# FFN1's up sets: one 512-column matmul per high weight block, with the main and cross halves added on DVE

## The chip, the core and the metric

The kernel runs on one NeuronCore of one Trainium2 chip. The metric is the device time of one execution in microseconds (us), as the median of several runs. Engine names are those of the profile: PE multiplies matrices and PEld loads its weights, DVE and ACT are the two elementwise engines that can read PE's accumulators, POOL and SP issue most of the DMAs.

## The reference

One transformer-like block on 512 tokens of width 1024, batch 1, float32: a first feed-forward layer (FFN1) with half weight, a mixer of a short causal convolution and a gated linear attention with their output projections, a second feed-forward layer (FFN2) with half weight, and a last normalisation. The part that the change concerns:

```python
D_MODEL, SEQ, D_FF = 1024, 512, 2816

def swiglu(x, w_gu, w_down):
    g, u = jnp.split(x @ w_gu, 2, axis=-1)
    return (jax.nn.silu(g) * u) @ w_down

x = x + 0.5 * swiglu(rmsnorm(x, norm_ffn1_g), ffn1_w_gu, ffn1_w_down)
x = x + hybrid_mixer(rmsnorm(x, norm_mix_g), w_in, conv_w, ...)
x = x + 0.5 * swiglu(rmsnorm(x, norm_ffn2_g), ffn2_w_gu, ffn2_w_down)
return rmsnorm(x, final_norm_g)
```

## The kernel before

**Numbers in two parts.** Every float32 operand of a matmul is split into a rounded high part and the remainder, the low part: ACT casts the value to the high part, DVE subtracts it from the value to get the low part. A product of two such operands is three matmuls into one accumulator: high weight by high operand, high weight by low operand, low weight by high operand. For weights the class `Weights` does this: a 128x1024 piece comes in by DMA (`f`), L358 casts it to `wh` on ACT, and L359 makes `wl` on DVE. `wh` and `wl` have 3 buffers each, so the cast for a product waits until the product three earlier has read its weights. L343 makes sums of weight pieces on DVE. For operands `Operands.make` does it (L599 on ACT, L600 on DVE).

**Sets.** Most large products are done in a Strassen-like way, with 7 half-size products instead of 8. A `Set` runs the products m1, p2, q6, p5, q7, p4 and p3. One product is 4 blocks of the contraction by 2 blocks of the output by the 3 matmuls above, 24 matmuls of 256 columns (L551) into one bank of the accumulator memory (PSUM). Bank b takes m1, q6, q7 and p4 one upon the other, bank a takes p2, bank c takes p5 and p3. After m1, q6 and q7 ACT copies bank b out (L556) before the next product adds into it. FFN1 and FFN2 have 9 such sets each in their up stage, with 4 pairs of plain column blocks ahead of them; the up stage's `done` then combines banks and copies on DVE (L715 after p2, L720 after q7, L724 after p4, L729 after p3). The down stages, the mixer's input projection and others use sets too, or plain runs of banks.

**Accumulators.** Eight banks in two pools: `ps` with 6 single banks given out by `MM()` (names `mm`), and `pa` with 2 given out by `AUX()` (names `aux`).

**What sets the order.** The program is written stage by stage; a scheduler of the framework then sets the order on each engine by its own cost estimates and adds the waits, from the tiles that an instruction reads and writes. A tile is the unit: an instruction that writes any part of a tile waits for earlier readers of any part of it. Only the last part of `last_down` is in written order (`manual_schedule`): for each of four token blocks t it runs `part(t, 0)` and `part(t, 1)`, 12 matmuls of 512 columns each (L833 to L835) into `o[t][0]` and `o[t][1]`, followed on DVE by the addition to the residual (L903), on ACT by squares, on DVE by the product with the last gain, and the store.

Of the kernel before, what the change touches and what calls it, by code (L numbers as in the profile page):

```python
# [78 lines left out]
HW = 256  # L79
# [136 lines left out]
def block_kernel(ctx: ExitStack, tc: tile.TileContext, xT, vecs, gf, gup, wgl, wts, out):  # L216
    nc = tc.nc
# [2 lines left out]

    front = ctx.enter_context(tc.tile_pool(name="front", bufs=1))
    keep = ctx.enter_context(tc.tile_pool(name="keep", bufs=1))
    ps = ctx.enter_context(tc.tile_pool(name="ps", bufs=6, space=bass.MemoryType.PSUM))
    pa = ctx.enter_context(tc.tile_pool(name="pa", bufs=2, space=bass.MemoryType.PSUM))

    cnt = [0]
# [11 lines left out]
    def tile_of(pool, shape, dtype=F32):  # L238
        cnt[0] += 1
        return pools[pool].tile(shape, dtype, tag=pool, name=f"{pool}{cnt[0]}")  # L240

    def T(dtype=F32):
        return tile_of("tp", [P, S], dtype)

    def MM():
        cnt[0] += 1
        return ps.tile([P, S], F32, tag="mm", name=f"mm{cnt[0]}")

    def AUX():
        cnt[0] += 1  # L250
        return pa.tile([P, S], F32, tag="aux", name=f"aux{cnt[0]}")
# [23 lines left out]
    class Weights:  # L275
# [3 lines left out]
        def __init__(self, ahead):  # L279
            self.ahead = ahead  # L280
            self.issued = 0
            self.taken = 0
            self.end = 0
            self.ready = []
            self.raw = {}
            self.loads = {}
            self.sums = {}
            self.pre = {}
# [88 lines left out]
    W = Weights(2)  # L377
# [145 lines left out]
    def mul(out_, a, b, eng=None):  # L523
        (eng or nc.vector).tensor_tensor(out=out_, in0=a, in1=b, op=ALU.mult)


    class Set:
# [8 lines left out]

        def run(self, p):
            b = {"m1": "b", "p2": "a", "q6": "b", "p5": "c", "q7": "b", "p4": "b", "p3": "c"}[p]
            fresh = b not in self.bank
            if fresh:  # L540
                self.bank[b] = MM()
            o = self.bank[b]
            bh, bl = self.group.get(p)
            h, l = W.take()
            for k in range(4):
                for e in range(2):
                    s = slice(k * HW + e * P, k * HW + (e + 1) * P)
                    t = slice(k * HW, (k + 1) * HW)
                    to = o[:, e * HW : (e + 1) * HW]
                    for j, (ww, aa) in enumerate(((h, bh), (h, bl), (l, bh))):  # L550
                        nc.tensor.matmul(to, ww[:, s], aa[:, t],  # L551
                                         start=fresh and k == 0 and e == 0 and j == 0,
                                         stop=k == 3 and j == 2, skip_group_check=True)
            if p in self.keep:
                v = T()
                nc.scalar.copy(v, o)  # L556
                self.v[p] = v
            self.done(self, p)

    class Operands:  # L560

        ORDER = ("m1", "p2", "p5", "q6", "q7", "p3", "p4")

        def __init__(self, b):
            self.b = b
            self.parts = {}
            self.sums = set()

# [19 lines left out]
        def make(self, p):  # L590
            if p in self.parts:
                return
            i = self.ORDER.index(p)
            if i > 0:
                self.make(self.ORDER[i - 1])
            v = self.sum(p)
            h, l = (tile_of("op", [P, 1024], F32R) for _ in range(2))
            hv, lv = (t.rearrange("p (k t) -> p k t", t=HW) for t in (h, l))
            nc.scalar.copy(hv, v)  # L599
            nc.vector.tensor_tensor(out=lv, in0=v, in1=hv.bitcast(F32), op=ALU.subtract)  # L600
            self.parts[p] = (h, l)
# [4 lines left out]
    class Tall:  # L606
# [7 lines left out]
        def run(self, p, s):  # L614
            b = {"p2": "a", "p5": "c", "p3": "c"}.get(p, "b")
            fresh = b not in self.bank
            if fresh:
                self.bank[b] = [MM(), MM()]
            bh, bl = self.group.get(p)
            h, l = W.take()  # L620
            for i in range(2):
                k = 2 * s + i
                wh, wl = (a[:, 512 * i : 512 * (i + 1)] for a in (h, l))
                for e in range(2):
                    c = slice(k * HW + e * P, k * HW + (e + 1) * P)
# [31 lines left out]
    def ffn(up, down, norm, nxt, plain, at):  # L657
# [7 lines left out]
        o = mm_group(up, KD, (0, DFF, P, DFF + P), xh, xl, extra=finish, slow=nxt is not None)  # L665
# [17 lines left out]
                xn[j, l] = v  # L683
            return xn[j, l]

        xo = Operands(normed)

        def plain_pair(f, g, u):
            s, t = T(), T()
# [9 lines left out]
        for f in range(2, plain):  # L699
# [5 lines left out]
                xo.sum("q6")  # L705
            plain_pair(f, g, u)

        def up_set(i):
            h = hid[:, plain + 2 * i : plain + 2 * i + 2]

            def done(s, p):
                bank, v = s.bank, s.v
                if p == "p2":
                    g1 = T()
                    nc.vector.tensor_tensor(out=g1, in0=bank["a"], in1=v["m1"], op=ALU.add)  # L715
                    nc.scalar.activation(g1, g1, AF.Silu)
                    s.g1 = g1
                if p == "q7":
                    u2 = T()
                    nc.vector.scalar_tensor_tensor(out=u2, in0=bank["c"], scalar=-1.0, in1=v["q7"],  # L720
                                                   op0=ALU.mult, op1=ALU.subtract)
                    s.u2 = u2
                if p == "p4":
                    nc.vector.scalar_tensor_tensor(  # L724
                        out=h[:, :, :HW], in0=pair(bank["b"]), scalar=-1.0, in1=pair(s.g1),
                        op0=ALU.mult, op1=ALU.mult)
                if p == "p3":
                    g2 = T()
                    nc.vector.tensor_tensor(out=g2, in0=bank["c"], in1=v["q6"], op=ALU.add)  # L729
                    nc.scalar.activation(g2, g2, AF.Silu)  # L730
                    mul(h[:, :, HW:], pair(s.u2), pair(g2))
                    if nxt is None and i < KD:
                        natural(i)

            return Set(xo, done)

        def pair(t):
            return t.rearrange("p (e t) -> p e t", t=HW)
# [13 lines left out]
            return last_down(us, hid, split_hid)  # L752

        def banks():
            return [AUX(), AUX()] + [MM() for _ in range(KD - 2)]

        def mm(d, k, w, hl):
# [10 lines left out]
        o = banks()  # L768
# [33 lines left out]
        o = banks()  # L802
# [17 lines left out]
    def last_down(us, hid, split_hid):  # L820
        X = XS[-1]
        gr = []
        for e in range(2):
            g = acc_row.tile([P, S], F32, tag=("acc", "row")[e], name=f"gr{e}")
            nc.sync.dma_start(g, gf[:, 512 * e : 512 * (e + 1)].to_broadcast([P, 512]))
            gr.append(g)

        o = [[MM(), MM()] for t in range(NTB - 1)] + [[AUX(), AUX()]]

        def mm(t, e, k, w, hl):  # L830
# [9 lines left out]
        def add(t, e, bank, by):  # L840
            xt = X[:, 4 * e : 4 * e + 4, t * P : (t + 1) * P]
            nc.vector.scalar_tensor_tensor(out=xt, in0=blocks(bank), scalar=by, in1=xt,
                                           op0=ALU.mult, op1=ALU.add)
# [25 lines left out]
        for p in CHUNK_ORDER:  # L869
            b = {"p2": "a", "p5": "c", "p3": "c"}.get(p, "b")  # L870
            fresh = b not in banks
            if fresh:
                banks[b] = [MM(), MM()]
            bh, bl = ho.get(p)
            for s in range(2):
                h, l = W.take()
                for i in range(2):
                    k = 2 * s + i
                    wh, wl = (a[:, 512 * i : 512 * (i + 1)] for a in (h, l))
                    for e in range(2):  # L880
                        c = slice(k * HW + e * P, k * HW + (e + 1) * P)
                        to = banks[b][e]
                        for n, (aa, ww) in enumerate(((bh, wh), (bh, wl), (bl, wh))):
                            nc.tensor.matmul(to, aa[:, c], ww,  # L884
                                             start=fresh and k == 0 and n == 0,
                                             stop=k == 3 and n == 2, skip_group_check=True)
            for l, e, by in uses[p]:
                for t in range(2):
                    add(2 * l + t, e, banks[b][t], by)
        o[:] = [[MM(), MM()] for t in range(NTB - 1)] + [[AUX(), AUX()]]  # L890
        w = [W.take(u) for u in us[KF - TAIL :]]
        hl = [split_hid(k) for k in range(KF - TAIL, KF, 2)]
# [41 lines left out]
        with tc.manual_schedule(engines={ENG.PE, ENG.DVE, ENG.Activation}):  # L934
# [4 lines left out]
            for t in range(NTB):  # L939
                sm = front.tile([P, 8], F32, tag="fin", name=f"fin{t}", bufs=2)  # L940
                f = [sm[:, i : i + 1] for i in range(6)]
# [563 lines left out]
```

## Time and profile before

| what | us |
|---|---|
| median of 3 runs (lowest, highest) | 1195.39 (1194.18, 1195.40) |
| the profiled execution's own time | 1195.04 |
| its span, first to last instruction | 1193.3 |
| PE busy in the span | 1183.7 |
| DVE busy | 841.7 |
| ACT busy | 591.7 |
| FFN1's up sets, from 50.46 to 232.43 | 181.97 |

The profile describes one execution, whose time was 1.74 us more than the span of its instructions. "Busy" adds up the instructions of an engine. A row of the timeline gives the start, the length, the engine, the line, the operation, the tiles written and read, and in brackets how long the engine sat idle before and what released it. Matmuls overlap in such rows, so the distance between the starts of two of them, not their length, tells what one costs. Buffer numbers are left out in the profile: `mm` is any bank of the pool `ps`.

### The profile page before, as it was taken

The page shows a single profiled execution, that of the slowest core. Times are in us where ns is not written, and L with a number is a line of the kernel's source. Part 1 is how long each engine was busy: PE and PEld are TensorE (multiplying, and loading weights), DVE is VectorE, ACT ScalarE, POOL GpSimd, SP SyncE. Part 2 cuts the span into 40 slices and gives each one's busy share as a digit, 9 for nine tenths or more (in the row PEclk, how much of TensorE's full clock was granted, in tenths as well). Part 3 has the DMA queues.
Part 4 walks back from the last instruction along what each step waited for, and adds up shares of the span by engine and source line. Part 5 has one row for each costly group of instructions (what it writes and reads, how often), then busy time and mean ns, then how long its engine had stood idle before and what let it go on. Part 6 is the DMA issues. An engine that isn't in the chain of part 4 may idle for free.

```text
span 1193.3 us, 19134 instructions
## 1 busy us (share of the span) xinstructions
PE 1183.7 (99%) x7834; PEld 1091.4 (91%) x7834; DVE 841.7 (71%) x1010; ACT 591.7 (50%) x736; POOL 106.4 (9%) x143
## 2 busy tenths in 40 slices
PE   9999999999999999999999999999999999999997
PEld 8899999988988889999999998888889999998886
DVE  7976666854787976667787786555597656675675
ACT  6554454622452746464554574334355555562353
POOL 0011111000110110101111100100001111100100
PEclk9999999999999999999999999999999999999999
DMA  9477777633482767778666766602637777763431
GB/s 345 82 210 183 189 177 190 182 89 90 99 278 72 172 158 208 196 185 212 143 152 147 189 172 214 203 18 78 213 81 211 170 184 173 185 174 117 92 92 70
DMA packets 58471, 190.80 MB, mean 160 GB/s; under 512 B 6576, under 2 KB 10800, under 8 KB 58384
## 3 DMA queue, kind: packets, MB, share of 16 engines
q1 hardware_dynamic: 36912, 124.27, 30.5%
q0 software_dynamic: 16832, 60.83, 27.5%
q10 hardware_dynamic: 4640, 4.49, 1.2%
q8 instruction: 61, 1.00, 0.3%
q14 instruction: 26, 0.21, 0.1%
HBM read 124.55 MB, written 8.39 MB: 111 GB/s over the span
## 4 chain that ended last, share of the span: by engine, by line
PE 97%; DVE 2%; issue 1%; ACT 0%; POOL 0%; DVEq 0%; ACTq 0%; POOLq 0%
PE mm L551 52%; PE mm L410 7%; PE mm L388 6%; PE mm L386 6%; PE mm L387 6%; PE mm L627 3%; PE mm L884 3%; PE mm L834 2%; PE mm L835 2%; PE mm L833 2%; PE aux L1173 1%; DVE wl L359 1%; PE aux L386 1%; PE aux L835 1%; PE aux L388 1%; PE aux L834 1%
## 5 line engine op out<-in xcount | busy, mean ns | idle before, releaser
L551 PE MATMUL mm<-op,wh 128*128 128x256 f32 x3584 | 648.8, 284 | 0.0
L358 ACT CAST wh<-f 128x1024 fp32r<-128x1024 f32 (+1 forms) x325 | 339.4, 1046 | 459.0 <-PE mm L551 221.8
L551 PEld LDWEIGHTS mm<-op,wh 128*128 128x128 f32 x3584 | 559.0, 192 | 1.1
L359 DVE TENSOR_TENSOR wl<-f,wh 128x1024 fp32r<-128x1024 f32 (+1 forms) x325 | 394.8, 1219 | 210.9 <-ACT wh L358 205.9
L551 PE MATMUL mm<-op,wl 128*128 128x256 f32 x1792 | 507.5, 283 | 0.9 <-DVE wl L359 0.9
L551 PEld LDWEIGHTS mm<-op,wl 128*128 128x128 f32 x1792 | 343.3, 192 | 1.6 <-DVE wl L359 1.5
L333 POOL DMA_DIRECT2D f<-f x108 | 93.4, 867 | 932.1 <-DVE wl L359 483.1
L386 PE MATMUL mm<-op,wh 128*128 128x512 f32 x340 | 132.3, 389 | 0.0
L387 PE MATMUL mm<-op,wh 128*128 128x512 f32 x340 | 132.3, 389 | 0.0
L388 PE MATMUL mm<-op,wl 128*128 128x512 f32 x340 | 132.3, 389 | 0.0
L387 PEld LDWEIGHTS mm<-op,wh 128*128 128x128 f32 x340 | 63.8, 188 | 13.3
L388 PEld LDWEIGHTS mm<-op,wl 128*128 128x128 f32 x340 | 63.8, 188 | 13.2
L386 PEld LDWEIGHTS mm<-op,wh 128*128 128x128 f32 x340 | 63.8, 188 | 13.2
L410 PE MATMUL mm<-op,wh 128*128 128x512 f32 x256 | 64.5, 394 | 0.0
L410 PEld LDWEIGHTS mm<-op,wh 128*128 128x128 f32 x256 | 48.6, 190 | 10.4
L556 ACT COPY tp<-mm 128x512 f32<-128x512 f32 x90 | 52.2, 580 | 2.0 <-DVE tp L1323 2.0
L599 ACT CAST op<-hid 128x1024 fp32r<-128x1024 f32 x28 | 29.4, 1051 | 37.4 <-PE aux L834 20.7
L600 DVE TENSOR_TENSOR op<-hid,op 128x1024 fp32r<-128x1024 f32 x28 | 34.2, 1222 | 17.7 <-ACT op L599 17.6
L343 DVE TENSOR_TENSOR f<-f,f 128x1024 f32<-128x1024 f32 x36 | 44.0, 1223 | 0.8
L627 PE MATMUL mm<-wh,op 128*128 128x512 f32 x112 | 34.9, 389 | 0.0
L884 PE MATMUL mm<-wh,op 128*128 128x512 f32 x112 | 34.6, 389 | 0.0
L410 PE MATMUL mm<-op,wl 128*128 128x512 f32 x128 | 34.2, 389 | 0.0
(252 smaller groups left out, 1107.7 us busy)
## 6 DMA issues: line engine op xcount, KB each, us to landing
f<-wts SPq DMA_DIRECT2D x219, 512.0 KB, 4.4
f<-f POOLq DMA_DIRECT2D x108, 512.0 KB, 5.0
X<-xT SPq DMA_DIRECT2D x8, 256.0 KB, 5.3
xs<-X POOLq DMA_DIRECT2D x8, 256.0 KB, 5.5
ga<-tp ACTq DMA_DIRECT2D x8, 256.0 KB, 5.3
gb<-tp ACTq DMA_DIRECT2D x8, 256.0 KB, 5.3
tp<-ga SPq DMA_DIRECT2D x8, 256.0 KB, 5.9
tp<-gb SPq DMA_DIRECT2D x8, 256.0 KB, 3.0
```

The costliest lines, as they stand in the source:

```text
L333: nc.gpsimd.dma_start(out_, a, accum_op=ALU.add)
L343: nc.vector.tensor_tensor(out=s3, in0=a11, in1=a21, op=ALU.add)
L358: nc.scalar.copy(h[:, :w], raw[:, :w])
L359: nc.vector.tensor_tensor(out=l[:, :w], in0=raw[:, :w], in1=h[:, :w].bitcast(F32), op=ALU.subtract)
L386: nc.tensor.matmul(o, wh, ah, start=first, stop=False)
L387: nc.tensor.matmul(o, wh, al, start=False, stop=False)
L388: nc.tensor.matmul(o, wl, ah, start=False, stop=last)
L410: nc.tensor.matmul(o[c], w[:, s : s + P], a[k], start=k == 0 and j == 0, stop=k == kt - 1 and j == 2)
L551: nc.tensor.matmul(to, ww[:, s], aa[:, t], start=fresh and k == 0 and e == 0 and j == 0, stop=k == 3 and j == 2, skip_group_check=True)
L556: nc.scalar.copy(v, o)
L627: nc.tensor.matmul(self.bank[b][e], aa[:, c], ww, start=fresh and i == 0 and n == 0, stop=k == 3 and n == 2, skip_group_check=True)
L884: nc.tensor.matmul(to, aa[:, c], ww, start=fresh and k == 0 and n == 0, stop=k == 3 and n == 2, skip_group_check=True)
```

## The change

In FFN1's up sets alone, an operand's high and low halves now lie beside each other, so that one matmul of 512 columns takes a high weight block to both of them. Its result is a main half (high by high) and a cross half (high by low), and the third matmul (low by high) adds into the cross half. A product is then 8 matmuls of 512 columns and 8 of 256, for each but p2, which keeps 24 matmuls of 256 columns in one bank of the pool `pa`. The accumulator of the others takes two banks. Where the kernel took bank b out by one ACT copy, `whole` now copies the cross half on ACT and adds the main half on DVE, after m1, q6, q7, and new after p4; after q7 and p3, where DVE combined one bank with a copy, it takes a second instruction for the cross half. That is six more DVE instructions of 512 elements and one more ACT copy for each set. An operand's split is done in two halves of 512 elements each instead of one piece of 1024.

The pool `ps` now has 3 tiles of two banks each instead of 6 of one. `MM2()` gives out such a tile, and `MM()`, which all other stages still call, gives out one half of a tile, then the other. The halves of one such tile are one tile to the waits.

```diff
-    ps = ctx.enter_context(tc.tile_pool(name="ps", bufs=6, space=bass.MemoryType.PSUM))
+    ps = ctx.enter_context(tc.tile_pool(name="ps", bufs=3, space=bass.MemoryType.PSUM))
...
+    half_bank = []
+
+    def MM2():
+        cnt[0] += 1
+        half_bank.clear()
+        return ps.tile([P, 2, S], F32, tag="mm", name=f"mm{cnt[0]}")
+
     def MM():
-        cnt[0] += 1
-        return ps.tile([P, S], F32, tag="mm", name=f"mm{cnt[0]}")
+        if half_bank:
+            return half_bank.pop()
+        t = MM2()
+        half_bank.append(t[:, 1])
+        return t[:, 0]
...
+        def run_joint(self, p, b):
+            fresh = b not in self.bank
+            two_banks = b != "a"
+            if fresh:
+                self.bank[b] = MM2() if two_banks else AUX()
...
+                    if two_banks:
+                        nc.tensor.matmul(o[:, e], h[:, s], a, start=fresh and k == 0,
+                                         stop=False, skip_group_check=True)
+                        nc.tensor.matmul(o[:, e, HW:], l[:, s], a[:, :HW], start=False,
+                                         stop=k == 3, skip_group_check=True)
+                        continue
...
+        def whole(self, b, v):
+            o = self.bank[b]
+            v = v.rearrange("p (e t) -> p e t", t=HW)
+            nc.scalar.copy(v, o[:, :, HW:])
+            nc.vector.tensor_tensor(out=v, in0=o[:, :, :HW], in1=v, op=ALU.add)
...
+            if self.joint:
+                t = [tile_of("op", [P, 1024], F32R) for _ in range(2)]
+                for i in range(2):
+                    a = t[i].rearrange("p (k b t) -> p k b t", b=2, t=HW)
+                    vi = v[:, 2 * i : 2 * i + 2]
+                    nc.scalar.copy(a[:, :, 0], vi)
+                    nc.vector.tensor_tensor(out=a[:, :, 1], in0=vi,
+                                            in1=a[:, :, 0].bitcast(F32), op=ALU.subtract)
...
                 if p == "q7":
-                    nc.vector.scalar_tensor_tensor(out=u2, in0=bank["c"], scalar=-1.0, in1=v["q7"],
+                    nc.vector.scalar_tensor_tensor(out=pair(s.u2), in0=main(bank["c"]),
...
+                    if xo.joint:
+                        nc.vector.tensor_tensor(out=pair(s.u2), in0=pair(s.u2),
+                                                in1=cross(bank["c"]), op=ALU.subtract)
                 if p == "p4":
...
+                    if xo.joint:
+                        s.whole("b", v["q7"])
...
+        half_bank.clear()
         o[:] = [[MM(), MM()] for t in range(NTB - 1)] + [[AUX(), AUX()]]
```

Three places show how the order of instructions moves. In the rows `op` tiles are operands, `wh` and `wl` are weights, `mm` and `aux` are accumulators, `tp` are copies in SBUF; the number in a name tells one tile from another, and a bracket names the engine whose earlier work the row waits for.

**FFN1's up sets, DVE.** Before, from the end of one set into the next:

```order
L359 TENSOR_TENSOR wl_1176<-f_908,wh_1175 128x1024
L720 SCALAR_TENSOR_TENSOR tp_1172<-mm_1104,tp_1170 128x512
L359 TENSOR_TENSOR wl_1207<-f_680,wh_1206 128x1024
L343 TENSOR_TENSOR f_1236<-f_1134,f_1138 128x1024
L724 SCALAR_TENSOR_TENSOR hid_353<-mm_946,tp_1039 128x2x256
L359 TENSOR_TENSOR wl_1240<-f_906,wh_1239 128x1024
L715 TENSOR_TENSOR tp_1267<-mm_1235,tp_1204 128x512
```

Now:

```order
L369 TENSOR_TENSOR wl_913<-f_415,wh_912 128x1024
L785 SCALAR_TENSOR_TENSOR tp_884<-mm_831,tp_881 128x512
L605 TENSOR_TENSOR tp_909<-mm_887,tp_909 128x512
L789 TENSOR_TENSOR tp_884<-tp_884,mm_831 128x512
L353 TENSOR_TENSOR f_936<-f_853,f_857 128x1024
L369 TENSOR_TENSOR wl_940<-f_666,wh_939 128x1024
L605 TENSOR_TENSOR tp_881<-mm_700,tp_881 128x512
L780 TENSOR_TENSOR tp_967<-aux_935,tp_909 128x512
L795 SCALAR_TENSOR_TENSOR hid_351<-tp_881,tp_780 128x2x256
```

Between the subtraction after q7 (L720 before, L785 now) and the addition after p2 (L715, L780) stand three more instructions of 512 elements: two additions of main halves (L605) and the second part of the subtraction (L789).

**FFN1's up sets, PE.** Before, each product is a run of 24 rows. Now the scheduler interleaves them: q6 and p5 as runs of 16, 5 rows of the next set's m1, q7's 16, the other 11 of m1, 8 rows of the next p2, p4's 16, the other 16 of p2, and p3's 16. The place where p2 begins, now:

```order
L585 MATMUL mm_1074<-op_357,wh_1019 128x512
L587 MATMUL mm_1074<-op_357,wl_1020 128x256
L593 MATMUL aux_1122<-op_372,wh_1075 128x256 [waits Activation_49]
L593 MATMUL aux_1122<-op_372,wh_1075 128x256
L593 MATMUL aux_1122<-op_372,wl_1076 128x256 [waits DVE_49]
```

The first two rows are the last of m1; p2's third row needs `wl_1076`, whose cast needs the weight buffer that q7 held until 11 rows earlier. Before, the 24 rows of m1 and the 24 of p4 stood between those two.

**The mixer's input sets, PE.** Before, at the start of a product that adds into a bank which ACT has to copy out first:

```order
L551 MATMUL mm_6363<-op_3898,wh_6286 128x256
L551 MATMUL mm_6363<-op_3899,wh_6286 128x256
L551 MATMUL mm_6363<-op_3898,wl_6287 128x256
L551 MATMUL mm_6105<-op_4258,wh_6331 128x256 [waits Activation_49]
L551 MATMUL mm_6105<-op_4259,wh_6331 128x256
```

Now, at a product with that same operand:

```order
L563 MATMUL mm_5463<-op_3776,wh_5597 128x256
L563 MATMUL mm_5463<-op_3777,wh_5597 128x256
L563 MATMUL mm_5463<-op_3776,wl_5598 128x256
L563 MATMUL mm_5780<-op_3565,wh_5720 128x256 [waits Activation_49]
L563 MATMUL mm_5780<-op_3566,wh_5720 128x256
L563 MATMUL mm_5463<-op_3883,wh_5681 128x256 [waits Activation_49]
L563 MATMUL mm_5463<-op_3884,wh_5681 128x256
```

Before, a whole product of 24 rows into another bank stands between the last row into `mm_6105` and the row that waits for its copy; now 2 rows stand there.

**The tail, PE.** The step from `part(1, 0)` to `part(1, 1)`, before:

```order
L833 MATMUL mm_11433<-op_11443,op_11451 128x512
L834 MATMUL mm_11433<-op_11444,op_11451 128x512
L835 MATMUL mm_11433<-op_11443,op_11452 128x512
L833 MATMUL mm_11434<-op_11397,op_11447 128x512 [waits PE_49]
L834 MATMUL mm_11434<-op_11398,op_11447 128x512
```

Now:

```order
L909 MATMUL mm_11004<-op_11012,op_11020 128x512
L910 MATMUL mm_11004<-op_11013,op_11020 128x512
L911 MATMUL mm_11004<-op_11012,op_11021 128x512
L909 MATMUL mm_11004<-op_10969,op_11016 128x512 [waits DVE_49]
L910 MATMUL mm_11004<-op_10970,op_11016 128x512
```

The two parts now write halves of one tile, and the second part's first row waits for DVE, which there reads the first part's half (the line that was L903 before).

More of the change, by code (lines that the diff above doesn't have):

```diff
@@ L538, in run @@
             b = {"m1": "b", "p2": "a", "q6": "b", "p5": "c", "q7": "b", "p4": "b", "p3": "c"}[p]
+            if self.group.joint:
+                return self.run_joint(p, b)
             fresh = b not in self.bank
@@ L558, in run, with __init__ @@
             self.done(self, p)
+        def run_joint(self, p, b):
[4 more added lines that the diff above has]
+            o = self.bank[b]
+            parts = self.group.get(p)
+            h, l = W.take()
+            for k in range(4):
+                a = parts[k // 2][:, (k % 2) * S : (k % 2 + 1) * S]
+                for e in range(2):
+                    s = slice(k * HW + e * P, k * HW + (e + 1) * P)
+                    if two_banks:
[4 more added lines that the diff above has]
+                        continue
+                    to = o[:, e * HW : (e + 1) * HW]
+                    for j, (ww, aa) in enumerate(((h, a[:, :HW]), (h, a[:, HW:]),
+                                                  (l, a[:, :HW]))):
+                        nc.tensor.matmul(to, ww[:, s], aa, start=k == 0 and e == 0 and j == 0,
+                                         stop=k == 3 and j == 2, skip_group_check=True)
+            if p in self.keep:
+                v = T()
+                self.whole(b, v)
+                self.v[p] = v
+            self.done(self, p)
+        def whole(self, b, v):
+            o = self.bank[b]
+            v = v.rearrange("p (e t) -> p e t", t=HW)
+            nc.scalar.copy(v, o[:, :, HW:])
+            nc.vector.tensor_tensor(out=v, in0=o[:, :, :HW], in1=v, op=ALU.add)
     class Operands:
         ORDER = ("m1", "p2", "p5", "q6", "q7", "p3", "p4")
-        def __init__(self, b):
+        def __init__(self, b, joint=False):
             self.b = b
+            self.joint = joint
             self.parts = {}
@@ L596, in make @@
             v = self.sum(p)
+            if self.joint:
[6 more added lines that the diff above has]
+                                            in1=a[:, :, 0].bitcast(F32), op=ALU.subtract)
+                self.parts[p] = t
+                return
             h, l = (tile_of("op", [P, 1024], F32R) for _ in range(2))
@@ L684, in normed @@
             return xn[j, l]
-        xo = Operands(normed)
+        xo = Operands(normed, joint=nxt is not None)
         def plain_pair(f, g, u):
@@ L706, in ffn, with main, cross @@
             plain_pair(f, g, u)
+        def main(t):
+            return t[:, :, :HW] if xo.joint else pair(t)
+        def cross(t):
+            return t[:, :, HW:]
         def up_set(i):
@@ L718, in done @@
                 if p == "q7":
-                    u2 = T()
-                    nc.vector.scalar_tensor_tensor(out=u2, in0=bank["c"], scalar=-1.0, in1=v["q7"],
+                    s.u2 = T()
+                    nc.vector.scalar_tensor_tensor(out=pair(s.u2), in0=main(bank["c"]),
+                                                   scalar=-1.0, in1=pair(v["q7"]),
                                                    op0=ALU.mult, op1=ALU.subtract)
-                    s.u2 = u2
+                    if xo.joint:
+                        nc.vector.tensor_tensor(out=pair(s.u2), in0=pair(s.u2),
+                                                in1=cross(bank["c"]), op=ALU.subtract)
                 if p == "p4":
-                    nc.vector.scalar_tensor_tensor(
-                        out=h[:, :, :HW], in0=pair(bank["b"]), scalar=-1.0, in1=pair(s.g1),
-                        op0=ALU.mult, op1=ALU.mult)
+                    b = pair(bank["b"]) if not xo.joint else pair(v["q7"])
+                    if xo.joint:
+                        s.whole("b", v["q7"])
+                    nc.vector.scalar_tensor_tensor(out=h[:, :, :HW], in0=b, scalar=-1.0,
+                                                   in1=pair(s.g1), op0=ALU.mult, op1=ALU.mult)
                 if p == "p3":
                     g2 = T()
-                    nc.vector.tensor_tensor(out=g2, in0=bank["c"], in1=v["q6"], op=ALU.add)
+                    nc.vector.tensor_tensor(out=pair(g2), in0=main(bank["c"]), in1=pair(v["q6"]),
+                                            op=ALU.add)
+                    if xo.joint:
+                        nc.vector.tensor_tensor(out=pair(g2), in0=pair(g2), in1=cross(bank["c"]),
+                                                op=ALU.add)
                     nc.scalar.activation(g2, g2, AF.Silu)
@@ L754, in banks @@
         def banks():
+            half_bank.clear()
             return [AUX(), AUX()] + [MM() for _ in range(KD - 2)]
@@ L826, in last_down @@
             gr.append(g)
+        half_bank.clear()
         o = [[MM(), MM()] for t in range(NTB - 1)] + [[AUX(), AUX()]]
@@ L872, in last_down @@
             if fresh:
+                half_bank.clear()
                 banks[b] = [MM(), MM()]
@@ L889, in last_down @@
                     add(2 * l + t, e, banks[b][t], by)
+        half_bank.clear()
         o[:] = [[MM(), MM()] for t in range(NTB - 1)] + [[AUX(), AUX()]]
```

## The prediction

> **What bounds the kernel now.** I read the page's engine sums and its chain first, then the groups, then the stage in which the matmuls change.
>
> ```profile
> PE 1183.7 (99%) x7834; PEld 1091.4 (91%) x7834; DVE 841.7 (71%) x1010; ACT 591.7 (50%) x736; POOL 106.4 (9%) x143
> PE 97%; DVE 2%; issue 1%; ACT 0%; POOL 0%; DVEq 0%; ACTq 0%; POOLq 0%
> L551 PE MATMUL mm<-op,wl 128*128 128x256 f32 x1792 | 507.5, 283 | 0.9 <-DVE wl L359 0.9
> L358 ACT CAST wh<-f 128x1024 fp32r<-128x1024 f32 (+1 forms) x325 | 339.4, 1046 | 459.0 <-PE mm L551 221.8
> L359 DVE TENSOR_TENSOR wl<-f,wh 128x1024 fp32r<-128x1024 f32 (+1 forms) x325 | 394.8, 1219 | 210.9 <-ACT wh L358 205.9
> ```
>
> PE is the bound all along: its rows fill 99% of the span, 97% of the chain is PE, and the one wait on DVE in the third row cost 0.9 us in the whole run. So a matmul saved is time saved, and every new wait of PE is time lost at full price. The last two rows show who feeds it: a cast of 1.05 us and a subtraction of 1.22 us for each weight piece. The stage itself, and two slices of it:
>
> ```profile
> core 0: us, PE busy (x) PEld busy (x) DVE busy (x) ACT busy (x) POOL busy (x), PEclk, DMA share, GB/s
> 50.46:232.43 181.97, 181.79 (x1514) 181.52 (x1512) 128.13 (x129) 98.21 (x118) 21.55 (x25) 1.00 0.74 184
> 50.46:70.60 20.14, 19.96 (x165) 19.69 (x164) 19.75 (x20) 14.03 (x17) 3.10 (x4) 1.00 0.72 184
> 90.80:111.00 20.20, 20.20 (x171) 20.20 (x170) 12.91 (x14) 9.86 (x12) 2.59 (x3) 1.00 0.75 183
> ```
>
> A set takes 20.2 us; DVE is busy for 12.9 of that in a steady set, but for 19.75 of 20.14 in the first one. The granted clock is 1.00 throughout.
>
> **The saving.** The price of a matmul is the distance of starts:
>
> ```profile
> 50.46 0.40 PE L551 MATMUL mm<-op,wh 128*128 128x256 f32 x2
> 50.69 0.28 PE L551 MATMUL mm<-op,wl 128*128 128x256 f32 x1
> 50.81 0.40 PE L551 MATMUL mm<-op,wh 128*128 128x256 f32 x2
> ...
> 1166.97 0.39 PE L833 MATMUL mm<-op,op 128*128 128x512 f32 x1
> 1169.69 0.39 PE L833 MATMUL mm<-op,op 128*128 128x512 f32 x1
> ```
>
> Three matmuls of 256 columns take 50.81 - 50.46 = 0.35 to 0.36, 0.12 each; the last two rows are 12 matmuls of 512 columns apart, 2.72 / 12 = 0.2267 each. Merging two of 256 into one of 512 saves 0.24 - 0.2267 = 0.0133. There are 9 sets x 6 products x 8 = 432 merges: 5.76 us. The stage's matmuls fall from 63 x 2.88 = 181.44 to 54 x 2.773 + 9 x 2.88 = 175.68.
>
> The Trainium skill ("TensorE: Matmul & The Clock Gate", section "Back-to-back issue gap") gives N/2.4 + 2.5 ns for N columns at the warm clock: 109.2 ns for 256, 215.8 for 512. By it a merge saves only 2.5 ns, all of them 1.1 us, and the sum below would be 4.7 us higher. This case's rows read 120 and 226.7, so I keep the rows.
>
> **What the up sets lose.** Distances that I need:
>
> ```profile
> 76.91 0.40 PE L551 MATMUL mm<-op,wh 128*128 128x256 f32 x2
> 77.04 1.05 ACT L358 CAST wh<-f 128x1024 fp32r<-128x1024 f32 x1 [1.36 <-PE mm L551]
> 77.11 0.69 DVE L729 TENSOR_TENSOR tp<-mm,tp 128x512 f32<-128x512 f32 x1 [0.69 <-PE mm L551]
> 78.00 0.63 ACT L730 ACTIVATE tp<-tp 128x512 f32<-128x512 f32 x1
> 78.12 1.23 DVE L359 TENSOR_TENSOR wl<-f,wh 128x1024 fp32r<-128x1024 f32 x1 [0.32 <-ACT wh L358]
> ...
> 57.03 0.39 PE L551 MATMUL mm<-op,wl 128*128 128x256 f32 x1 [0.18 <-DVE wl L359]
> 57.25 0.40 PE L551 MATMUL mm<-op,wh 128*128 128x256 f32 x2
> ```
>
> A product ends at 76.91, where the next starts: the cast into its buffer begins 0.13 later, DVE's read of its bank 0.20 later; `wl` begins 0.03 after the cast's end (78.09 to 78.12). When PE waits for `wl`, its next matmul comes 0.22 after the late one instead of 0.12, so I count 0.14 from DVE's end to PE at speed.
>
> Steady sets: DVE gets six operations of 0.69 more, 12.9 + 4.1 = 17.0 of some 20 us, which fits on average, as does ACT's one copy more. But p2's third matmul now waits for a chain that starts at q7's end: 0.13 + 1.05 + 0.03 + 1.23 + 0.14 = 2.58, and PE has 11 rows of m1 (5 x 0.2267 + 6 x 0.12 = 1.85) and two of p2 (0.24) to cover it: 0.49 lost in each of six sets, with some 0.1 more for q7, whose bank must now pass a copy and an addition. That is 3.4. A late set adds about 1.3, where p4 stands directly behind 11 rows and needs copy and addition behind a weight subtraction. First set: DVE is full before the change (19.75 of 20.14) and gets 4 us of work more, so up to 4 are lost; I take 3.0, since the additions after p4 and p3 fall into the next slice, where DVE has 7 us free. Sum lost 7.7; the 0.5 that PE lost here before goes. Stage: 175.7 + 7.7 = 183.4 against 181.97, **+1.4** (bounds -2.5, if the first set recovers and the steady chain hides, and +4).
>
> **What the pairs of banks cost elsewhere.** FFN1's down sets: the second product into a bank now stands 2 rows behind the first, and waits until DVE's addition has read it.
>
> ```profile
> 300.24 1.22 DVE L359 TENSOR_TENSOR wl<-f,wh 128x1024 fp32r<-128x1024 f32 x1
> 301.37 0.69 DVE L796 SCALAR_TENSOR_TENSOR X<-mm,X 128x512 f32<-128x512 f32 x1
> 300.61 0.40 PE L551 MATMUL mm<-op,wh 128*128 128x256 f32 x2
> ```
>
> The first product ended at 300.61, where its successor starts, and the addition, behind a `wl`, at 302.06: 302.06 + 0.14 - 300.61 - 0.24 = 1.35. The sets after it have 8 rows of cover, 0.07 each. At FFN1's end, three pairs of plain banks finish one behind the other, and one of them waits for its twin's addition: 0.20 + 0.69 + 0.14 = 1.03, as in the tail below. With 0.2 for the small ones, **+2.6** (1.3 to 3.5).
>
> Mixer and FFN2: at four places in the mixer's sets, and two in FFN2's up sets, 0 or 2 rows stand where a whole product stood between the last matmul into a bank and the next one that adds into it. PE then waits for ACT's copy, which stands in ACT's order behind a cast that gets ready at the same moment:
>
> ```profile
> 620.87 1.05 ACT L358 CAST wh<-f 128x1024 fp32r<-128x1024 f32 x1 [1.78 <-PE mm L551]
> 621.83 0.58 ACT L556 COPY tp<-mm 128x512 f32<-128x512 f32 x1
> ```
>
> From the cast's start to the copy's end it is 622.41 - 620.87 = 1.54, with 0.13 ahead and 0.14 behind 1.81; less 2 rows, 1.57. If the cast were done, it is 0.20 + 0.58 + 0.14 = 0.92, less 0.24: 0.68. Mixer: 1.57 twice and 1.81 twice is 6.8, low 3.2; nearer the high end, because the quoted rows show that very pair back to back. I take 5.5 with some 0.5 of small ones in it. FFN2: 2 x 1.57, low 1.4; I take 2.6. The output projections and single banks, which now share a tile two by two, wait some 8 times for a read of the twin (1.03 as in the tail), of which rows into other banks cover all but about 0.1: 0.8. Together **+8.9** (5.2 to 11.4).
>
> The tail: `part(t, 1)` waits for DVE's reading of `part(t, 0)` for t = 0, 1, 2.
>
> ```profile
> 1167.17 0.69 DVE L903 SCALAR_TENSOR_TENSOR X<-mm,X 128x512 f32<-128x512 f32 x1 [2.03 <-PE mm L835]
> 1167.90 0.69 DVE L524 TENSOR_TENSOR tp<-X,gr 128x512 f32<-128x512 f32 x1
> ```
>
> `part(0, 0)` ended at 1166.97; 0.20 + 0.69 + 0.14 = 1.03 each, three times **+3.1**, with nothing to cover it: PE is in written order there and ends the program. t = 3 has its own tiles and keeps its pace. The order of SP and POOL is unchanged, so the transfers cost nothing new; casts that move with PE's products only move their issue along.
>
> **Sum.** 1195.0 (the profiled execution; the median is 0.35 higher) + 1.4 + 2.6 + 8.9 + 3.1 = 1211.0. The bounds add to -2.5 + 1.3 + 5.2 + 3.1 = +7.1 and 4 + 3.5 + 11.4 + 3.2 = +22.1.
>
> **Rivals.** (1) The pairs' waits hide, because DVE and ACT come to their reads earlier than I read from the trace of before, and the up sets keep the saving: only the tail's 3.1 stays, 1195.0 - 5.8 + 3.1 = 1192.3, or 1189.3 if even the tail's read came in time. For it: DVE is idle 29% of the span. Against: a read cannot start before the product's end plus 0.20, and the tail row was released by PE itself, so 0.92 to 1.03 stands wherever no row covers it. The point at which it decides: fewer than 5.8 us of waits in all. (2) The up sets give back just the saving and elsewhere all copies find their engine free: 1195 + 0 + 1.3 + 5.2 + 3.1 = 1204.6. (3) DVE becomes the bound of the up sets: if each set's DVE work (17.0) is in the order of the products' needs and not free to slide, each addition queues behind a `wl` of 1.22, twice a set, 9 x 2 x 1.22 = 22 minus what I have counted (7.7) = 14 more: 1225. Against it: 3 us a set are idle. (4) The merge saves only the 1.1 us of the page's rule: 1215.7. Against it: the rows' 0.0133.
>
> **Chances.** My sum, within its range of 1204 to 1217: 0.72. Rival 2 and what lies near it down to 1198: 0.08. Rival 4 and moderate queueing, 1217 to 1221: 0.08. Rival 3: 0.05. Rival 1: 0.05, and 0.02 for ends within 0.2% (2.4 us) of before, which is about what a measurement of this kernel can tell from no change. Slower 0.93, same 0.02, faster 0.05. The predicted time is 1210.5, half a microsecond under the sum, since a wait that lets DVE catch up spares the next. Range 1202 to 1219.
>
> **What the profile after would show.** Starts of 512- and 256-column rows alternating at 0.2267 and 0.12 in the up sets; a stage of 181 to 186 us, its first set the longest; PE idle of 15 to 25 us in the whole run, put down to DVE additions and ACT copies outside the up sets; in the tail three gaps of 1.0 us ahead of `part(t, 1)` and none for t = 3. I am wrong if PE idles for less than 8 us, or if the stage ends under 178 us.

## The result, and the profile after

The changed kernel takes 1224.16 us (median of 4 runs, 1223.46 to 1224.57) against 1194.95 for the kernel before beside it: a ratio of 1.0245, 95% interval 1.0227 to 1.0262. It is slower by 29.2 us. The forecast was slower, at 1210.5 in a range of 1202 to 1219: the direction was right, and the size was about half of what came.

The page of the profiled execution (1223.91 us, span 1222.2), its sums by engine and its chain:

```profile
PE 1191.9 (98%) x7402; PEld 1067.6 (87%) x7402; DVE 869.5 (71%) x1071; ACT 597.8 (49%) x752; POOL 106.2 (9%) x143
PE 89%; DVE 5%; ACT 3%; DMA 2%; issue 2%; SPq 0%; ACTq 0%; DVEq 0%
```

PE has 432 matmuls fewer and its busy time is 8 us longer, so busy time tells little here. The chain tells more: PE's share fell from 97% to 89%, and DVE and ACT stand in it with 8%. PE's waits, with what ended them (total us, times, longest):

```profile
PE mm L563 <- ACT wh L368: 6.1, 6, 1.6
PE mm L909 <- DVE X L981: 2.4, 3, 0.8
PE mm L585 <- DVE tp L605: 2.3, 2, 1.3
PE mm L563 <- ACT tp L568: 2.2, 2, 1.5
PE aux L593 <- DVE wl L369: 1.4, 6, 0.2
...
PE mm L396 <- DVE y L534: 1.1, 1, 1.1
PE mm L686 <- DVE wl L369: 1.1, 1, 1.1
PE aux L593 <- ACT wh L368: 1.0, 1, 1.0
PE mm L420 <- DVE X L838: 0.9, 1, 0.9
PE mm L398 <- DVE wl L369: 0.7, 1, 0.7
```

L585, L587 and L593 are the matmuls of FFN1's up sets, where the change was made. Most of the waits are at other lines: L563 is the set matmul of the mixer, of FFN1's down and FFN2's up stage, L909 the tail. In windows by stage, before:

```profile
core 0: us, PE busy (x) PEld busy (x) DVE busy (x) ACT busy (x) POOL busy (x), PEclk, DMA share, GB/s
232.43:297.74 65.31, 65.31 (x291) 54.06 (x290) 34.19 (x34) 18.92 (x20) 3.45 (x4) 1.00 0.37 101
297.74:338.05 40.31, 40.31 (x338) 40.31 (x337) 29.24 (x32) 16.54 (x16) 3.44 (x5) 1.00 0.48 124
432.76:712.25 279.49, 278.29 (x2247) 272.86 (x2246) 206.78 (x257) 158.36 (x206) 29.75 (x38) 1.00 0.69 176
886.85:1071.75 184.90, 184.90 (x1546) 184.89 (x1545) 126.95 (x128) 101.97 (x126) 21.52 (x25) 1.00 0.74 182
1164.25:1193.30 29.05, 21.92 (x97) 17.83 (x95) 17.41 (x46) 9.54 (x24) 0.00 (x0) 0.91 0.19 72
```

And after:

```profile
50.45:236.57 186.12, 181.05 (x1083) 158.60 (x1082) 156.34 (x185) 102.25 (x130) 21.51 (x25) 1.00 0.71 179
236.57:301.42 64.85, 64.85 (x288) 53.68 (x287) 36.31 (x36) 19.96 (x21) 3.44 (x4) 1.00 0.40 106
301.42:343.42 42.00, 40.98 (x337) 40.57 (x336) 28.82 (x32) 16.44 (x16) 3.44 (x5) 1.00 0.44 108
440.66:727.85 287.19, 280.72 (x2248) 273.60 (x2246) 207.78 (x260) 158.76 (x206) 29.66 (x38) 1.00 0.67 171
906.12:1099.29 193.17, 190.16 (x1554) 187.34 (x1553) 128.95 (x131) 102.26 (x126) 21.50 (x25) 1.00 0.71 178
1189.81:1222.20 32.39, 22.89 (x97) 17.60 (x95) 17.81 (x46) 9.54 (x24) 0.00 (x0) 0.96 0.17 66
```

The up sets and the banks behind them (which interlock by two rows after) take 250.97 instead of 247.28, **+3.7**. FFN1's down sets: **+1.7**. From their end to the mixer's sets 97.24 instead of 94.71, **+2.5**. The mixer's sets: **+7.7**. From their end to FFN2's sets 178.27 instead of 174.60, **+3.7**. FFN2's sets: 193.17 holds 9 rows of the next stage (9 x 0.227 = 2.0), so **+6.2**. The banks after them +0.1, and the tail **+3.3**. That is 28.9, the difference of the spans. Only 3.7 of it lie where the arithmetic was changed.

### The profile page after: what moved, and what is told of

It is laid out like the page before. It is cut to its first block, busy times and chain, and to the rows that moved or that the text cites. A ratio compares the mean times of both kernels' runs of the same rounds, so it can differ in the third digit from the quotient of the medians.

```text
span 1222.2 us, 18379 instructions
## 1 busy us (share of the span) xinstructions
PE 1191.9 (98%) x7402; PEld 1067.6 (87%) x7402; DVE 869.5 (71%) x1071; ACT 597.8 (49%) x752; POOL 106.2 (9%) x143
## 4 chain that ended last, share of the span: by engine, by line
PE 89%; DVE 5%; ACT 3%; DMA 2%; issue 2%; SPq 0%; ACTq 0%; DVEq 0%
PE mm L563 36%; PE mm L420 7%; PE mm L585 7%; PE mm L396 6%; PE mm L398 6%; PE mm L397 6%; PE mm L587 3%; PE mm L961 3%; PE mm L686 3%; DVE wl L369 2%; ACT wh L368 2%; PE aux L593 2%; PE mm L909 2%; PE mm L911 2%; PE mm L910 2%
## 5 line engine op out<-in xcount | busy, mean ns | idle before, releaser
L563 PE MATMUL mm<-op,wh 128*128 128x256 f32 x2576 | 471.2, 285 | 9.9 <-ACT wh L368 6.1
L563 PEld LDWEIGHTS mm<-op,wh 128*128 128x128 f32 x2576 | 401.8, 191 | 16.2 <-ACT wh L368 8.8
L563 PE MATMUL mm<-op,wl 128*128 128x256 f32 x1288 | 361.9, 283 | 0.6 <-DVE wl L369 0.6
L563 PEld LDWEIGHTS mm<-op,wl 128*128 128x128 f32 x1288 | 245.3, 191 | 1.0 <-DVE wl L369 0.8
L585 PE MATMUL mm<-op,wh 128*128 128x512 f32 x432 | 152.7, 398 | 2.7 <-DVE tp L605 2.3
L396 PE MATMUL mm<-op,wh 128*128 128x512 f32 x340 | 132.5, 392 | 1.1 <-DVE y L534 1.1
L398 PE MATMUL mm<-op,wl 128*128 128x512 f32 x340 | 132.2, 390 | 0.7 <-DVE wl L369 0.7
L397 PE MATMUL mm<-op,wh 128*128 128x512 f32 x340 | 132.4, 389 | 0.0
L587 PE MATMUL mm<-op,wl 128*128 128x256 f32 x432 | 119.4, 280 | 0.0
L585 PEld LDWEIGHTS mm<-op,wh 128*128 128x128 f32 x432 | 81.0, 188 | 22.4 <-DVE tp L605 3.0
L587 PEld LDWEIGHTS mm<-op,wl 128*128 128x128 f32 x432 | 81.5, 189 | 0.5
L396 PEld LDWEIGHTS mm<-op,wh 128*128 128x128 f32 x340 | 63.8, 188 | 17.0 <-DVE y L534 2.4
L398 PEld LDWEIGHTS mm<-op,wl 128*128 128x128 f32 x340 | 63.8, 188 | 14.6 <-DVE wl L369 1.1
L397 PEld LDWEIGHTS mm<-op,wh 128*128 128x128 f32 x340 | 63.8, 188 | 12.9
L420 PE MATMUL mm<-op,wh 128*128 128x512 f32 x256 | 64.4, 391 | 1.3 <-DVE X L838 0.9
L420 PEld LDWEIGHTS mm<-op,wh 128*128 128x128 f32 x256 | 47.7, 188 | 12.4 <-issue 1.3
L658 DVE TENSOR_TENSOR op<-hid,op 128x1024 fp32r<-128x1024 f32 x21 | 25.6, 1221 | 18.5 <-ACT op L657 18.5
L568 ACT COPY tp<-mm 128x512 f32<-128x512 f32 x63 | 36.5, 579 | 2.2 <-DVE tp L1401 1.7
```

The costliest lines, as they stand in the source:

```text
L396: nc.tensor.matmul(o, wh, ah, start=first, stop=False)
L397: nc.tensor.matmul(o, wh, al, start=False, stop=False)
L398: nc.tensor.matmul(o, wl, ah, start=False, stop=last)
L420: nc.tensor.matmul(o[c], w[:, s : s + P], a[k], start=k == 0 and j == 0, stop=k == kt - 1 and j == 2)
L563: nc.tensor.matmul(to, ww[:, s], aa[:, t], start=fresh and k == 0 and e == 0 and j == 0, stop=k == 3 and j == 2, skip_group_check=True)
L585: nc.tensor.matmul(o[:, e], h[:, s], a, start=fresh and k == 0, stop=False, skip_group_check=True)
```

## The experiments

Each was timed beside the kernel before on the same chip, whose medians were 1194.4 to 1194.8. Theory A: the loss is PE's waits where two banks share one tile, each stage losing its own. Theory B: the merged matmuls upset the order, and the later waits follow from that.

### Pairs of banks, no merged matmuls

```diff
-        xo = Operands(normed, joint=nxt is not None)
+        xo = Operands(normed)
```

> The pairs of banks stay everywhere, the up sets of FFN1 go back to 24 matmuls of 256 columns. Theory A (the loss lies in waits between the two halves of a pair, outside the up sets): 1195 plus what the stages behind the up sets lost in the trace after (1.7 + 1.4 + 1.2 in FFN1's end and the mixer's start, 7.7 in the mixer's sets, 3.7 in the output projections, 6.2 in FFN2's sets, 3.3 in the tail = 25.2), so about 1220. Theory B (the merged matmuls upset the order and the later waits follow from them): close to 1195, at most 1200.

Measured: 1231.09 (ratio 1.0311, interval 1.0296 to 1.0326), **+36.5**, more than the whole change. Theory B falls. PE's waits in this run:

```profile
PE mm L563 <- ACT wh L368: 11.3, 11, 1.6
PE mm L563 <- ACT tp L568: 3.8, 3, 1.7
PE mm L909 <- DVE X L981: 2.4, 3, 0.8
PE mm L396 <- DVE y L534: 1.6, 1, 1.6
```

The expectation was 11 too low because it left FFN1's own up sets out: there, too, ordinary sets lie in pairs in this run, and lose 10 us. From 49.84 the sets run to 241.9 when the next stage's rows are taken off, 192.1 against 181.97. So in the changed kernel the merged form even spared some of what pairs cost.

### Merged matmuls, single banks everywhere else

```diff
+    def banks_by(n):
+        if psum:
+            psum["stack"].close()
+        stack = ExitStack()
+        psum.update(n=n, stack=stack, ps=stack.enter_context(tc.tile_pool(
+            name=..., bufs=6 // n, space=bass.MemoryType.PSUM, reuse_waits="tile")))
...
+        if nxt is not None:
+            banks_by(2)
         run_sets(up_set)
+        if nxt is not None:
+            banks_by(1)
```

> The merged matmuls stay in the up sets of FFN1, with three tiles of two banks there alone; ahead of them and behind them the pool has six single banks as before the change. Theory A: only what the up sets lost stays, +3.7, so about 1199 (up to 1201 if the two changes of the pool cost a wait). Theory B: the later waits stay too, 1215 to 1224.

Measured: 1197.17 (ratio 1.0023, interval 1.0013 to 1.0032), **+2.5**. PE's waits:

```profile
PE mm L602 <- DVE wl L384: 1.3, 1, 1.3
PE aux L285 <- POOL ones L282: 1.1, 1, 1.1
PE aux L608 <- DVE wl L384: 1.1, 5, 0.2
PE mm L600 <- DVE tp L620: 1.1, 1, 1.1
PE mm L578 <- DVE wl L384: 0.7, 2, 0.6
PE aux L1229 <- DVE qk L549: 0.5, 1, 0.5
PE mm L600 <- DVE tp L804: 0.4, 1, 0.4
```

L600, L602 and L608 are in the up sets. The others are the waits of the kernel before. That is 1.2 less than the expected 3.7: the first set lost 1.7 us here, by the starts, where it had lost 2.9. So 26.7 of the 29.2 us are the price of dealing the accumulator banks in pairs outside the changed stage, and the merged form by itself loses 2.5 in its own.

### The tail with the pairs dealt crosswise

```diff
-        o[:] = [[MM(), MM()] for t in range(NTB - 1)] + [[AUX(), AUX()]]
+        first, second = ([MM() for t in range(NTB - 1)] for e in range(2))
+        o[:] = [[first[t], second[t]] for t in range(NTB - 1)] + [[AUX(), AUX()]]
```

> The changed kernel, but in the tail the pairs are dealt crosswise, so that the two parts of one token block lie in different tiles and a tile's second half is written three parts after its first. Theory A: the three gaps ahead of the second parts go, 3 x 1.1 = 3.3, so about 1221, with nothing else moved. If DVE's reads bound the tail anyway: 1224, with the gaps at another place.

Measured: 1221.30 (ratio 1.0223, interval 1.0208 to 1.0238), 2.9 below the changed kernel. The tail takes 29.07 from its first matmul to the end (29.05 before, 32.39 in the changed kernel), and the line "PE mm L909 <- DVE X L981" is gone from its waits, while those of the sets, 6.1 for casts and 2.2 for copies, stand as they were. The same pool, the same tiles, and only which two accumulators share one: the tail's waits are made by the sharing.

### High weights first

```diff
+            for low in range(2):
+                for k in range(4):
...
+                        if two_banks and low:
+                            nc.tensor.matmul(to[:, HW:], l[:, s], a[:, :HW], ...)
+                        elif two_banks:
+                            nc.tensor.matmul(to, h[:, s], a, ...)
```

> As the run with single banks outside the up sets, and within each product of FFN1's up sets all matmuls with the high weight first, then all with the low one. In the trace after, a merged matmul and the one with the low weight behind it took 0.353 together, not 0.2267 + 0.12 = 0.347. If the alternation of lengths costs that, blocks of one length bring 432 x 0.006 = 2.7 back, and the low weight is wanted 1.8 later, so that the six waits of 0.49 at p2 go too: about 1199 - 2.7 - 2.9 = 1193.5. If the longer merged matmul costs it in any order: 1196. If the waits come from the copy and addition of bank b and not from the low weight: 1196 to 1199.

Measured: 1194.08 (ratio 0.9996, interval 0.9987 to 1.0006), the same as before, and 3.1 below the run without it. The waits at p2 (five of 0.47 in the run without it) are gone; six delays of 0.17 ahead of L605 are left, too short for the profile's idle time and seen in the starts alone. The lengths tell about the other half. In most products of the changed kernel a pair takes a third of 101.03 - 99.97, 0.353:

```profile
99.97 0.40 PE L585 MATMUL mm<-op,wh 128*128 128x512 f32 x1
100.20 0.28 PE L587 MATMUL mm<-op,wl 128*128 128x256 f32 x1
...
101.03 0.40 PE L585 MATMUL mm<-op,wh 128*128 128x512 f32 x1
```

In blocks, eight of each:

```profile
105.58 2.00 PE L605 MATMUL mm<-op,wh 128*128 128x512 f32 x8
107.42 1.11 PE L602 MATMUL mm<-op,wl 128*128 128x256 f32 x8
108.38 0.40 PE L605 MATMUL mm<-op,wh 128*128 128x512 f32 x1
```

Eight pairs take 108.38 - 105.58 = 2.80, 0.350 each. So blocks gave back about half of what this pace costs over 0.347: 432 x 0.003 = 1.3. What still waited was in the first set (0.55, 0.39 and 0.74 us at L605, on DVE) and at the last (1.99 at L411, on ACT's cast of a weight). These four include the slow row behind each wait: the first one took 0.11 longer than its like.

### Merged only in the seven middle sets

```diff
+            merged = xo.joint and 0 < i < 8
...
+            return Set(xo, done, merged=merged)
```

> As the run with the high weights first and single banks elsewhere, but the first and the last of FFN1's nine up sets are done with 24 matmuls of 256 columns and without the extra work on DVE. If what that run still lost (0.57 + 0.41 + 0.76 in the first set, 2.0 at the last) is DVE's work in the two sets where it was full before the change, these 3.8 go, and two ninths of the saving (about 0.8) with them: 1194.1 - 3.8 + 0.8 + 0.5 for the waits of before = 1191.6. If the waits come from weights or from the order and not from DVE's added work: 1194 to 1195.

Measured: 1192.03 (ratio 0.9977, interval 0.9969 to 0.9986), faster than the kernel before by 0.2%. The profile counts no idle PE in the stage (179.16 of 179.16, against a stage of 181.97 before; the six delays of 0.17 are still there):

```profile
50.32:229.48 179.16, 179.16 (x1177) 164.09 (x1176) 151.72 (x175) 102.89 (x130) 21.52 (x25) 1.00 0.74 187
```

### DVE's additions left out

```diff
             nc.scalar.copy(v, o[:, :, HW:])
-            nc.vector.tensor_tensor(out=v, in0=o[:, :, :HW], in1=v, op=ALU.add)
```

> As the run with the high weights first and single banks elsewhere, and DVE's additions of the main halves after m1, q6, q7 and p4 are left out (the result lacks them), 36 instructions of 0.69. If DVE's load makes the waits in the first and the last set: these 3.8 shrink to under 1.5, about 1191.5. If they come from elsewhere (the splits, the weights): no change, 1194.

Measured: 1190.53 (ratio 0.9964, interval 0.9950 to 0.9977), 3.5 below the run with them. The first set's 1.7 us shrink to 0.2, the six delays of 0.17 go, and the last set's 2.0 shrink to 1.3, of which 1.0 stands behind ACT's copy. With the run before it this shows that DVE's added work caused the loss of the first set. At the last set the additions account for a third; the rest goes with the merge, but which part of the merge makes it is not shown.

### Pairs from FFN2's up sets on, no merged matmuls

```diff
-        if nxt is not None:
+        if nxt is None:
             banks_by(2)
         run_sets(up_set)
```

> No merged matmul anywhere; single banks up to FFN2's up sets, and from there on the three tiles of two banks. If each stage's loss is its own (theory A), FFN2's up sets lose the 6.2 and the tail the 3.3 that they lost in the changed kernel: 1194.6 + 9.5 = 1204. If the later stages lose because earlier ones shifted, 1195 to 1199.

Measured: 1208.32 (ratio 1.0113, interval 1.0099 to 1.0127), **+13.6**, with nothing changed ahead of those sets. Theory A's kind of loss, but 4 more than expected. The sets lost 7.9 instead of 6.2, and 2.2 came ahead of them, at the change of the pool: nine transposes that stood inside the sets before (1.0) and a wait of 1.2 for ACT's copy of a transposed block. Nine transposes inside the sets are worth 0.8 (before, 32 of them took 2.8), so like for like the sets lost 8.7.

### The same, with a tile of its own for each bank of FFN2's up sets

```diff
-                self.bank[b] = MM()
+                self.bank[b] = MM() if psum["n"] == 1 else MM2()[:, 0]
```

> As the run with pairs from FFN2's up sets on, but in those sets each bank takes a tile of two banks for itself and leaves the second half unused, so that no two banks share a tile while there are still only three tiles. If the sharing of a tile makes the waits: the 10 us that FFN2's sets lost there go and the tail's 3.2 stay, 1194.7 + 3.2 = about 1198. If three tiles are too few, with or without sharing: 1205 to 1209.

Measured: 1200.12 (ratio 1.0049, interval 1.0035 to 1.0062). The sets and the tail:

```profile
889.09:1074.47 185.38, 185.38 (x1536) 184.33 (x1537) 124.25 (x126) 100.31 (x123) 20.63 (x24) 1.00 0.72 183
1166.98:1199.36 32.38, 22.88 (x97) 17.59 (x95) 17.79 (x46) 9.54 (x24) 0.00 (x0) 0.92 0.17 65
```

The sets are down to 185.38 (184.90 before), with as few tiles as in the run above. With the nine transposes ahead of them counted, they lose 1.3 where sharing lost 8.7. So here three tiles are nearly enough, and it is the sharing that costs; for the mixer's sets and the projections this is inferred from the same kind of wait, since no run gave those stages tiles of their own. The 2.2 ahead of the sets stayed, which the expectation had missed, and the tail's 3.3.

### Merged in the middle sets of both layers

```diff
-        xo = Operands(normed, joint=nxt is not None)
+        xo = Operands(normed, joint=True)
```

> As the run with the middle sets of FFN1, and the same done in FFN2's middle sets. The run in FFN1 brought 2.7. In FFN2's up sets PE also transposes, through the two tiles of the pool that p2 now takes its bank from. If DVE's free time is what decides: another 2 to 2.7, 1189.5 to 1190. If p2 and the transposes now wait for each other's tiles, 8 transposes at up to 1 us each take it back: 1192 to 1197.

Measured: 1189.47 (ratio 0.9959, interval 0.9945 to 0.9973), the fastest: 4.9 below the kernel before. FFN2's sets take 182.57 instead of 184.90, again without idle PE:

```profile
883.57:1066.14 182.57, 182.57 (x1210) 167.58 (x1208) 150.84 (x174) 107.44 (x138) 21.49 (x25) 1.00 0.74 184
```

## Why the prediction was wrong

**The saving** was mis-sized: 5.76 was forecast from 0.2267 and 0.12 for a pair, and 3.6 came. The alternation runs at two paces. In some products a pair takes just the forecast 0.347, a third of 107.61 - 106.57:

```profile
106.57 0.39 PE L585 MATMUL mm<-op,wh 128*128 128x512 f32 x1
...
107.61 0.39 PE L585 MATMUL mm<-op,wh 128*128 128x512 f32 x1
```

In most it takes 0.353, as at 99.97 above. Of 309 stretches of three pairs that no wait disturbs, 59 ran at the fast pace, and the others took 0.353 on average. With the waits taken out, the 432 pairs average 0.3516, so a merge saved 0.36 - 0.3516 = 0.0084, all of them 3.6. Both prices were right for rows among their like, but their sum held for one stretch in five, and no row of before showed the two lengths side by side. The Trainium skill's rule ("TensorE: Matmul & The Clock Gate", section "Back-to-back issue gap"), which that section gives for a matmul by itself, had made it 0.0025. The measured value lies between the two, so **Rival 4**, a saving of 1.1, did not come either.

**What the up sets lose** was right in sum: 7.7 us were forecast, and the starts show 7.9, the slow row behind each wait included. The 0.49 at p2 in six sets was 0.47 to 0.50, the late set's 1.3 was 1.34, and the first set's 3.0 was 2.9. The 0.5 for q7 did not come, and 0.65 at the stage's end, which I had not forecast, stands in its place: to that extent the sum agrees by luck. That DVE was full in the first set was the right reading, as the runs with the middle sets merged and without the additions show. The stage came to 7.9 - 3.6 - 0.5 = +3.8 (by the windows +3.7) instead of +1.4, nearly all because of the saving.

**The tail** was right: 3.1 forecast, 3.3 measured, three gaps ahead of `part(t, 1)` and none for t = 3:

```profile
1192.30 0.39 PE L911 MATMUL mm<-op,op 128*128 128x512 f32 x1
1193.47 0.50 PE L909 MATMUL mm<-op,op 128*128 128x512 f32 x1 [0.78 <-DVE X L981]
1193.81 0.40 PE L910 MATMUL mm<-op,op 128*128 128x512 f32 x1
```

**FFN1's down sets** were right too (1.6 and 1.7), with the row that waited for DVE's addition 0.05 behind its end; the stretch to the mixer's sets less so: of its 2.5, I had 1.0 at FFN1's end, which came, and not a wait of 1.2 for a `wl` at L686.

**The step that failed is the count of the places in "Mixer and FFN2" with the output projections, +8.9.** They cost 7.7 + 6.2 + 3.7 = 17.6. The mechanism stood as forecast, also its price: at 1048.68, where two rows of a new bank stand between two products of one bank,

```profile
1047.59 1.04 ACT L368 CAST wh<-f 128x1024 fp32r<-128x1024 f32 x1 [1.79 <-PE mm L563]
1048.54 0.58 ACT L568 COPY tp<-mm 128x512 f32<-128x512 f32 x1
...
1047.39 0.28 PE L563 MATMUL mm<-op,wl 128*128 128x256 f32 x1
1048.68 0.99 PE L563 MATMUL mm<-op,wh 128*128 128x256 f32 x4 [1.02 <-ACT wh L368]
...
1049.17 0.30 PEld L563 LDWEIGHTS mm<-op,wh 128*128 128x128 f32 x2 [0.19 <-ACT tp L568]
```

PE loses 1.18 ahead of the row and 0.34 in the four rows from there, 1.52 where the forecast had 1.57. There are two waits in it. The long one ends with the cast of the two rows' own weight, in a buffer that the product just ahead had held. The third of the four rows then waits for the copy: its weights are loaded from 1049.17, 0.05 after the copy's end at 1049.12 (PEld's row). So the copy behind a cast decides, as I wrote, though the profile's list names the cast alone.

In FFN2 I counted two such places. The trace has six gaps there: two at this price (1.52 and 1.57), one of 0.5 at the end, and three of 0.65 to 0.9 at transposes, where the copy is waited for in the same way:

```profile
922.90 0.30 PEld L563 LDWEIGHTS mm<-op,wh 128*128 128x128 f32 x2 [0.64 <-ACT wh L368]
923.39 0.30 PEld L563 LDWEIGHTS mm<-op,wh 128*128 128x128 f32 x2 [0.19 <-ACT tp L568]
```

In the mixer I counted four, and the trace has eight gaps: four large ones that end in a wait for a copy, 6.3 in all where I took 5.0, and four of 0.4 to 0.8, 2.7 in all, for copies, DVE's reads and a weight, where I had 0.5; 2.0 of waits of the kernel before went. In the projections I had 0.1 for each shared pair and it was 0.15 seven times, but 1.35 for `y` and 1.0 for a `wl` came on top, which are waits for an operand and a weight.

**Rival 3**, DVE as the bound of the up sets, did not come: the time lies within a microsecond of its 1225, but by chance, since the up sets lost 7.9 and not 22. **Rival 1**, that waits hide, was wrong: the places that I had counted lost about their full price.

Left open: why the scheduler's order put a weight's cast late at L686 and L398. These waits go when the banks are single again, but no run took one of them alone. Also why a change of the pool ahead of FFN2's sets moved nine transposes ahead of them and made a wait of 1.2 us.

## What to carry to other kernels

Where a scheduler tracks accumulators by tile, a tile of two banks is a lock on both: give two banks one tile only where the same instructions use both, and single ones elsewhere, by phase if need be. Where an edit moves work from the bounding engine to another, look at that engine slice by slice: here DVE had room in seven sets of nine, and leaving out the two in which it was fullest (19.75 of 20.14 us, and 17.74 of 20.60) turned no gain into 2.7 us. To count what a new order costs, follow each row's every wait, the weight's cast as well as the accumulator's copy.

## What the runs showed of the hardware

A matmul of 512 columns is not 0.2267 everywhere. In alternation with 256 columns it took 0.235 on average over the 432 of the changed kernel, and the 256 behind it 0.117; a pair took 0.347 in some stretches and 0.353 in most. In blocks of eight behind a block of 256, the first ones took 0.233, 0.236, 0.229, 0.232 and 0.231, and the rest 0.227. After a wait, too, PE does not start at speed: in the tail the first matmul behind the gap took 0.335 and the next three 0.235, and in the sets of 256 columns the row behind a wait took 0.22 instead of 0.12. What in PE makes this was not tested.
